# Expert weights of a pair in runs of 16 KiB, the second pair ranked beside `up`, and late transposes in the attention of a hybrid trunk

## The chip, the core and the metric

The kernel runs on one core of one Trainium2 chip. A core has five engines with queues of their own: TensorE (PE, with its weight loads as PEld), VectorE (DVE), ScalarE (ACT), GpSimd (POOL) and SyncE (SP), which here only issues transfers, and 16 DMA engines that carry them. The metric is the device time of one execution in microseconds; the number that counts is the median of repeated executions.

## What is computed

The reference is an encoder trunk of two layers on 512 tokens of 1024 values, all in float32. Cut to what matters:

```python
for i in range(DEPTH):                       # 2 layers
    proj = rmsnorm(h, g_mix[i]) @ w_in[i]    # 1024 x 2816: q, k, v of three head groups
    oa = axial_gqa(...)                      # a: 4 query heads, 2 key heads, normed and rotated q, k
    ob = neighbourhood_attn(...)             # b: 6 heads, 2-D window, learned bias
    oc = dilated_mixture(...)                # c: 6 heads, three dilated windows
    h = h + concat(rmsnorm each group) @ w_out[i]
    h = h + expert_choice_ffn(rmsnorm(h, g_ffn[i]), ...)
    h = h + sigmoid(rmsnorm(h, g_ple[i]) @ w_ple_gate[i]) * (p[i] @ w_ple_proj[i])

def expert_choice_ffn(h, w_router, w_gate, w_up, w_down):
    aff = softmax(h @ w_router)              # 16 experts
    gates, idx = top_k(aff.T, 64)            # each expert picks 64 tokens
    hid = silu(h[idx] @ w_gate) * (h[idx] @ w_up)     # 1024 x 1024 each, per expert
    return segment_sum((hid @ w_down) * gates, idx)
```

The weights of the experts are 3 x 16 matrices of 4 MiB in each layer, read once: 201 MB per layer. That is most of what the kernel loads.

## The kernel before

A layer goes through three stages. In **attention** the projection of the 2816 columns is cut into seven blocks in the order `cq, ck, cv, a, bq, bk, bv` (`IN_BLOCKS`, L36). A block is a `Project` (L355): eight steps of 128 input values, four token tiles in each, three products per step and tile, since operands are split into a high and a low half for the fast float32 format (`split`, L321: ACT makes the high half, POOL the low one). Work of VectorE and ScalarE is hung on the steps of a block by a dictionary from step to functions that `run` (L392) takes. So `post_qk` (L532) hands the norm and rotation of the q or k heads of the block before to steps 0 to 7 of this one: `chain` at step 0 makes the factors, `norm(t)` works on token tile t in place in the tile `raw` (four buffers, filled by `fin_qk`, L524, with a square and a copy on ACT), and `tr(t)` transposes the heads of tile t on PE into a buffer of the pair. `norm` has its operations in program order (`in_turn`, L513, its line in the profile is L515). Between the products of a block the units of the attention before it are emitted by `Side` (L167): each unit has a cost in microseconds, `step` grants credit for every product group at a pace, and `LEAD` (L42) is a cost that must be paid before the first unit of a group comes out. A scheduler then orders what is not pinned.

The **experts** work in eight pairs. For a pair, `gate`, `up` and `down` are four steps each (`expert_mm`, L1071); a step has 16 products of 64 columns by 512, the two experts j = 0, 1 in the two halves of the array. A pair's tokens are found by `choose` (L1044: `rank`, eight transposes of the affinities on PE and eight comparisons on VectorE, then four `pick`), `number` (L1022: the tokens' indices and gates by four products, each two matmul instructions in the trace) and `bring` (L1051: `number`, then an indirect transfer of the tokens' rows). Pair 0 instead gathers with products of one-hot matrices (`fetch`, L1036, the instructions `pick,h`). In pair 0, `number(0)` and `choose(1)` are done at gate step 2 and `bring(1)` at up step 1. The embedding stage follows, with `w_ple_gate` in four pieces.

All weights and many other long-lived tiles live in `Slots` (L89): 18 buffers of 8 KiB per partition, and in the expert stage three more lent from the pool `phY` (`NEARLY`, from the last part of the out-projection on) and two from `phX` (`NLENT`). A list made by `plan` (L244) gives the order of the loads. `pump` (L121) issues on SP whatever stands first as long as a buffer is free beyond a reserve, which `keep` (L134) sets at several points of attention (`KEEP`, L45); an expert load may also take a lent buffer. SP issues in order: a load whose buffer is not free yet, or whose completion counter (one of eight, used in turn) is still held by the eighth load before it, keeps those behind it waiting. One load of expert weights is a piece of two input blocks of one expert's matrix, 1 MiB, 8 KiB per partition in one run; a step needs two of them (j = 0, 1):

```python
for name, w in (("g", w_gate), ("u", w_up), ("d", w_down)):
    for i in range(4):
        for j in range(2):
            slots.want((l, name, e + j, i), [(lambda t: t, w[l, e + j, i])])
```

In the listing all products have the line of the helper `mm` (L210) and all transposes that of `transpose` (L213), so the profile tells them apart by their tiles.

## Time and profile before

| what | before |
|---|---|
| median of three executions | 1638.31 us |
| the three executions | 1637.62, 1638.31, 1642.08 us |
| the profiled execution | 1637.69 us |
| its span in the profile | 1635.9 us |
| PE busy | 1537.8 us (94%) |
| VectorE, ScalarE, GpSimd busy | 722.1, 474.9, 277.6 us |
| moved by DMA | 469.85 MB, mean 287 GB/s |
| loads of expert weights | 384 of 1024 KB, 19.8 us each from issue to landing |

The profiled execution's time is 1.8 us more than its span, which runs from the first to the last instruction. PE is busy most of the time, but a mean over stages hides that they have different limits: the slices of the page show 20 to 150 GB/s in attention and about 420 in the two expert stages. A busy PE also need not be PE at its peak, as the ends of matmuls are modelled. The time from issue to landing of a load contains the loads ahead of it in the DMA engines' queues. "x" and a number at the end of a timeline row counts the instructions merged into it, and a bracket gives the time for which the engine stood idle before, with what ended it.

### The profile page before, as it was taken

The numbers are of one execution on the slowest core, as the hardware profiler recorded it, in microseconds if no ns is written. First come the engines' busy times: TensorE is split into PE (matmuls) and PEld (weight loads), VectorE is DVE, ScalarE is ACT, GpSimd is POOL, SyncE is SP. The second block draws the span as 40 slices with busy tenths as digits, with TensorE's granted clock in tenths as the row PEclk, the third lists the DMA queues.
The fourth block names the chain that finished last, engine by engine and source line by source line (L and its number), as shares of the span: only waits on it lengthen the run. The fifth ranks groups of instructions, "written<-read, shape, count | busy, mean of one in ns | idle before, by whom it ended". The sixth has DMA issues, their size and how long they took to land.

```text
span 1635.9 us, 20629 instructions
## 1 busy us (share of the span) xinstructions
PE 1537.8 (94%) x7819; PEld 884.3 (54%) x7819; DVE 722.1 (44%) x1909; ACT 474.9 (29%) x1127; POOL 277.6 (17%) x282
## 2 busy tenths in 40 slices
PE   7999999899999888998999999998999997889988
PEld 7866777644343333333897667776344333333346
DVE  4767756443243222222476687554333242122143
ACT  6455544211010002012564645541101010021034
POOL 3413364000000000000443233620000000000013
PEclk9999999999999999999999999999999999999999
DMA  9103146899999999999420032387999999999961
GB/s 323 39 20 104 24 150 239 324 385 420 420 420 421 420 421 399 421 421 421 166 73 20 20 103 58 116 333 290 422 420 420 421 420 421 421 397 421 419 279 52
DMA packets 74691, 469.85 MB, mean 287 GB/s; under 512 B 10272, under 2 KB 13280, under 8 KB 23392
## 3 DMA queue, kind: packets, MB, share of 16 engines
q1 hardware_dynamic: 69808, 454.16, 69.5%
q0 software_dynamic: 3744, 13.16, 2.2%
q10 hardware_dynamic: 1040, 1.21, 0.3%
q8 instruction: 61, 1.00, 0.2%
q14 instruction: 38, 0.31, 0.1%
HBM read 461.04 MB, written 6.29 MB: 286 GB/s over the span
## 4 chain that ended last, share of the span: by engine, by line
PE 51%; DMA 32%; DVE 12%; ACT 3%; issue 1%; POOL 1%; SPq 0%; POOLq 0%; ACTq 0%; DVEq 0%
PE bank L210 47%; DMA slot<-in_w_up_dram 11%; DMA slot<-in_w_gate_dram 7%; DMA slot<-in_w_down_dram 7%; PE bank L213 4%; DVE raw L515 4%; DMA slot<-in_w_ple_proj_dram 3%; DMA slot<-in_w_ple_gate_dram 2%; DVE p L661 2%; DVE w L515 1%; DVE p L654 1%; ACT p L656 1%; DMA slot<-in_w_in_dram 1%; DMA gain<-in_qk_gain_dram 1%; DVE slot L682 1%
## 5 line engine op out<-in xcount | busy, mean ns | idle before, releaser
L210 PE MATMUL bank<-slot,xt 128*64 128x512 f32 x2048 | 464.7, 595 | 29.5 <-DMA slot<-in_w_up_dram 23.6
L210 PE MATMUL bank<-ch,slot 128*128 128x384 f32 (+1 forms) x2064 | 477.9, 374 | 2.1 <-DVE slot L332 1.8
L210 PEld LDWEIGHTS bank<-ch,slot 128*128 128x128 f32 x2064 | 361.0, 190 | 77.1 <-issue 40.2
L210 PEld LDWEIGHTS bank<-slot,xt 128*64 128x64 f32 x2048 | 147.4, 137 | 320.2 <-issue 260.6
L327 POOL TENSOR_TENSOR ch<-slot,ch 128x384 fp32r<-128x384 f32 (+1 forms) x172 | 200.0, 1169 | 351.2 <-ACT ch L326 341.4
L210 PE MATMUL bank<-slot,hid 128*64 128x512 f32 x1024 | 229.2, 595 | 13.9 <-DMA slot<-in_w_down_dram 10.9
L210 PEld LDWEIGHTS bank<-slot,hid 128*64 128x64 f32 x1024 | 76.0, 137 | 156.2 <-issue 125.9
L1165 DVE SCALAR_TENSOR_TENSOR hid<-bank,st,hid 128x512 f32<-128x512 f32 x32 | 24.0, 751 | 304.4 <-PE bank L210 302.5
L1055 POOL DMA_INDIRECT xg<-rows,ids x14 | 13.6, 971 | 727.5 <-DVE ids L1028 637.6
L210 PE MATMUL bank<-slot,slot 128*64 128x256 f32 (+4 forms) x688 | 129.1, 420 | 3.6 <-DVE sa L654 1.9
L326 ACT CAST ch<-slot 128x384 fp32r<-128x384 f32 (+1 forms) x172 | 95.8, 563 | 85.8 <-PE bank L210 68.9
L1202 DVE SCALAR_TENSOR_TENSOR xg<-bank,st,hid 128x512 fp32r<-128x512 f32 x32 | 22.6, 746 | 215.8 <-ACT hid L1201 215.8
L1100 DVE TENSOR_TENSOR h<-h,bank 128x512 f32<-128x512 f32 x128 | 79.8, 682 | 82.7 <-PE bank L210 82.7
L1161 ACT ACTIVATE hid<-bank,st 128x512 f32<-128x512 f32 x32 | 22.0, 687 | 264.5 <-PE bank L210 264.5
L210 PEld LDWEIGHTS bank<-slot,slot 128*64 128x64 f32 (+2 forms) x688 | 63.1, 160 | 50.9 <-issue 26.3
L1006 DVE SCALAR_TENSOR_TENSOR less<-bank,tgv,order 128x512 bf16<-128x512 f32 x128 | 87.6, 747 | 3.9 <-PE bank L213 3.9
L1067 ACT ACTIVATE xt<-bank,gcols 128x128 f32<-128x128 f32 x56 | 20.3, 367 | 213.5 <-PE bank L213 211.8
L1201 ACT ACTIVATE hid<-bank,st 128x512 fp32r<-128x512 f32 x32 | 20.2, 683 | 211.9 <-issue 145.4
L656 ACT ACTIVATE p<-p,sa 128x512 f32<-128x512 f32 (+1 forms) x96 | 58.7, 612 | 69.0 <-DVE sa L654 68.8
L332 DVE SCALAR_TENSOR_TENSOR slot<-bank,gcols,slot 128x128 fp32r<-128x128 f32 (+1 forms) x160 | 53.0, 372 | 42.2 <-ACT slot L331 42.0
L213 PE MATMUL bank<-ident,p 128*128 128x128 f32 x416 | 62.4, 273 | 5.1 <-ACT ot L720 3.0
L654 DVE CUSTOM_DVE_ANT_0 p<-bank,slot 128x512 f32<-128x512 f32 (+1 forms) x96 | 50.8, 549 | 35.4 <-PE bank L210 27.2
(135 smaller groups left out, 1384.7 us busy)
## 6 DMA issues: line engine op xcount, KB each, us to landing
slot<-in_w_gate_dram SPq DMA_DIRECT2D x128, 1024.0 KB, 19.8
slot<-in_w_up_dram SPq DMA_DIRECT2D x128, 1024.0 KB, 19.8
slot<-in_w_down_dram SPq DMA_DIRECT2D x128, 1024.0 KB, 19.8
slot<-in_w_in_dram SPq DMA_DIRECT2D x24, 768.0 KB, 15.0
slot<-in_w_ple_gate_dram SPq DMA_DIRECT2D x8, 1024.0 KB, 19.8
slot<-in_w_out_dram SPq DMA_DIRECT2D x6, 1024.0 KB, 6.4
slot<-in_w_in_dram SPq DMA_DIRECT2D x4, 1024.0 KB, 5.1
rows<-h POOLq DMA_DIRECT2D x8, 512.0 KB, 4.8
```

What stands on the lines that cost most here:

```text
L210: return placed(T.matmul(*a, **k))
L213: return placed(T.transpose(*a))
L326: S.copy(hi.bitcast(F32R), src)
L327: G.tensor_tensor(lo.bitcast(F32R), src, hi, ALU.subtract)
L332: V.scalar_tensor_tensor(lo.bitcast(F32R), b, g, hi, ALU.mult, ALU.subtract)
L515: tc.keep_in_program_order(V.tensor_tensor(*a))
L654: V.tensor_tensor_reduce(pv, in0=sv, in1=bias, scale=-1.0, scalar=3e38, op0=ALU.add, op1=ALU.min, accum_out=nm)
L656: S.activation(pv, pv, AF.Exp, bias=nm, scale=-1.0, accum_out=ls)
L661: V.tensor_scalar(pv, pv, r[:, i:i + 1], None, ALU.mult)
L1006: V.scalar_tensor_tensor(ph.pool.tile([128, 512], BF16, tag="less", name="less", bufs=2), bk[6 + j], aff[:, t, e:e + 1], order[:, 128 * (3 ...
L1100: V.tensor_tensor(h[:, t, 512 * c:512 * c + 512], h[:, t, 512 * c:512 * c + 512], b, ALU.add)
L1165: V.scalar_tensor_tensor(hid[:, c], bk[2 + c], rslot[:, pr:pr + 1], hid[:, c], ALU.mult, ALU.mult)
```

## The change

Three things are changed. First, the expert weights are laid out in DRAM by pair, so that one load brings step i of both experts, 2 MiB, with 16 KiB per partition in one run. `Slots` therefore holds nine buffers of 16 KiB, and one each from the two lent pools; other users get a half of such a buffer (`piece`), of a buffer that is opened either for loads and plain tiles (`f32`) or for tiles that hold rounded halves (`rounded`), and the buffer is free when both halves are. `keep` counts halves, with new reserves. Second, `choose(1)` moves from gate step 2 of pair 0 to up step 1, `number(0)` to gate step 3 and `bring(1)` to up step 2. Third, `post_qk` returns two dictionaries: `tr(2)` is at step 7 instead of 6, and `tr(3)` at step 1 of the block after; the numbers of `LEAD` grow.

```diff
@@ -39,12 +39,13 @@
 
 PACE = (1.0, 0.85, 0.8)
 
-LEAD = (0.5, 2.0, 3.0)
+LEAD = (3.5, 4.0, 4.0)
 BIAS_AT = 5
-
-KEEP = (9, 3, 2, 4)
-
-NEARLY, NLENT = 3, 2
+FIRST = 6
+
+KEEP = (11, 3, 2, 4)
+
+NEARLY, NLENT = 1, 1
 
 EMBED = 5
 
@@ -94,7 +95,8 @@
         self.nc = nc
         self.pool = pool
         self.lent = {}
-        self.free = list(range(NSLOT))
+        self.free = list(range(NSLOT // 2))
+        self.open = {}
         self.where = {}
         self.queue = []
         self.ready = {}
@@ -115,18 +117,29 @@
             self.free.remove(i)
         self.lent = {}
 
+    def fresh(self, i):
+        self.free.remove(i)
+        return self.lent.get(i, self.pool).tile([128, 2 * SLOT], F32, tag=f"slots{i}", name=f"slots{i}", bufs=1)
+
     def own(self):
-        return [i for i in self.free if i < NSLOT]
+
+        n = 2 * sum(i not in self.lent for i in self.free)
+        return n + sum(len(halves) for _, kind, halves in self.open.values() if kind == "f32")
 
     def pump(self):
         while self.queue and self.queue[0][0][0] <= self.layer:
-            ok = self.own() if len(self.own()) > self.reserve else []
+            spare = self.own() - self.reserve
             if self.queue[0][0][1] in ("g", "u", "d"):
-                ok = [i for i in self.free if i >= NSLOT or i in ok]
-            if not ok:
+                ok = [i for i in self.free if i in self.lent or spare > 1]
+                if not ok:
+                    return
+                t = self.fresh(ok[0])
+                self.where[id(t)] = (ok[0], None, t)
+            elif spare > 0:
+                t = self.piece("f32")
+            else:
                 return
             key, loads = self.queue.pop(0)
-            t = self.tile(ok[0])
             for view, src in loads:
                 self.nc.sync.dma_start(out=view(t), in_=src)
             self.ready[key] = t
@@ -147,20 +160,32 @@
     def done(self, key):
         self.give(self.ready.pop(key))
 
-    def tile(self, i):
-        self.free.remove(i)
-        t = self.lent.get(i, self.pool).tile([128, SLOT], F32, tag=f"slot{i}", name=f"slot{i}", bufs=1)
-        self.where[id(t)] = (i, t)
+    def piece(self, kind):
+        ok = [i for i, (_, k, halves) in self.open.items() if k == kind and halves]
+        if not ok:
+            ok = [i for i in self.free if i not in self.lent]
+            self.open[ok[0]] = (self.fresh(ok[0]), kind, [0, 1])
+        big, _, halves = self.open[ok[0]]
+        s = halves.pop(0)
+        t = big[:, SLOT * s:SLOT * s + SLOT]
+        self.where[id(t)] = (ok[0], s, t)
         return t
 
-    def take(self):
+    def take(self, kind="f32"):
         if self.reserve:
             self.reserve -= 1
-        return self.tile(self.own()[0])
+        return self.piece(kind)
 
     def give(self, *tiles):
         for t in tiles:
-            self.free.append(self.where.pop(id(t))[0])
+            i, s, _ = self.where.pop(id(t))
+            if s is not None:
+                halves = self.open[i][2]
+                halves.append(s)
+                if len(halves) < 2:
+                    continue
+                del self.open[i]
+            self.free.append(i)
         self.pump()
 
 
@@ -268,8 +293,7 @@
                 chunks(("pp",), w_ple_proj[l])
             for name, w in (("g", w_gate), ("u", w_up), ("d", w_down)):
                 for i in range(4):
-                    for j in range(2):
-                        slots.want((l, name, e + j, i), [(lambda t: t, w[l, e + j, i])])
+                    slots.want((l, name, e, i), [(lambda t: t, w[l, e // 2, i])])
         chunks(("ple",), w_ple_gate[l])
 
     ph = Phase("init")
...
@@ -585,7 +610,7 @@
                     V.tensor_copy(d, four(b)[:, 0:nh // 2, :])
 
             return {0: [chain], 1: [lambda: norm(0)], 2: [lambda: norm(1)], 3: [lambda: norm(2)],
-                    4: [lambda: norm(3), lambda: tr(0)], 5: [lambda: tr(1)], 6: [lambda: tr(2)], 7: [lambda: tr(3)]}
+                    4: [lambda: norm(3), lambda: tr(0)], 5: [lambda: tr(1)], 7: [lambda: tr(2)]}, {1: [lambda: tr(3)]}
 
         def fin_v(c0, dst):
             n = dst.shape[2]
@@ -705,9 +730,9 @@
                                self.pt(hp, s)[:, 256 * c:256 * c + 256], start=c == 0, stop=c == 3)
                 k = groups[self.kind][0] // 128 + pr["j"]
                 if k not in mt:
-                    if len(mt) % 2 == 0:
-                        mts.append(slots.take())
-                    u = four(mts[-1])
+                    if not mts:
+                        mts.extend(slots.take('rounded') for _ in range(4))
+                    u = four(mts[len(mt) // 2])
                     mt[k] = (u[:, 2 * (len(mt) % 2), :], u[:, 2 * (len(mt) % 2) + 1, :])
                 if self.kind not in og:
                     og[self.kind] = ph.tile(512, "squares")
@@ -774,13 +799,15 @@
         pj["cq"].run({4: [stats_h]}, pj["ck"])
         pinned[0] = False
         cqk = [slots.take()]
-        pj["ck"].run(post_qk(6, 0, 4, "c", 0, cqk[0]), pj["cv"])
+        now, late = post_qk(6, 0, 4, "c", 0, cqk[0])
+        pj["ck"].run(now, pj["cv"])
         cqk.append(slots.take())
         vct = slots.take()
         vc = vct[:, 0:1536].rearrange("q (t c) -> q t c", t=4)
         va = pa.tile(512, "va").rearrange("q (t c) -> q t c", t=4)
         layer.fin["cv"] = fin_v(0, vc)
-        pj["cv"].run(merge(post_qk(0, 6, 4, "c", 1, cqk[1]), {7: [gains_h]}), pj["a"])
+        now, then = post_qk(0, 6, 4, "c", 1, cqk[1])
+        pj["cv"].run(merge(late, now, {7: [gains_h]}), pj["a"])
         logn = slots.take()
         nc.sync.dma_start(out=four(logn), in_=cst_logn.rearrange("q (t k) -> q t k", t=4))
         ptx = [slots.take() for _ in range(2)]
...
@@ -857,7 +886,8 @@
             bias["fin"](t)
 
         layer.fin["bv"] = fin_vb
-        pj["bv"].run(merge(post_qk(0, 6, 2, "b", 0, bqk[1]), {BIAS_AT: [bias_b]}))
+        now, late = post_qk(0, 6, 2, "b", 0, bqk[1])
+        pj["bv"].run(merge(then, now, {BIAS_AT: [bias_b]}))
         vb = bias["v"]
         vsh = [ptx[1][:, 384 * i:384 * i + 384] for i in range(3)]
         for i in range(3):
@@ -940,9 +970,9 @@
               out_project("b", (2, 3, 4), 0, MAIN),
               out_project("b", (2, 3, 4), 1, FREE, last=(3, 4), fin=tail)]
         for i in range(4):
-            po[i].run(None, po[i + 1])
+            po[i].run(None if i else late, po[i + 1])
             if i % 2:
-                slots.give(mts.pop(0))
+                slots.give(mts[i // 2])
         side.drain()
         pa.close()
         phY = Phase("early", "right")
...
@@ -1072,15 +1102,14 @@
             for i in range(4):
                 for f in (at or {}).get(i, ()):
                     f()
-                ws = [slots.get((l, name, e + j, i)).rearrange("q (k f) -> q k f", k=2) for j in range(2)]
+                ws = slots.get((l, name, e, i)).rearrange("q (j k f) -> q j k f", j=2, k=2)
                 for kk in range(2):
                     k = 2 * i + kk
                     for c in range(2):
                         for j in range(2):
-                            mm(bk[banks[c]][64 * j:64 * j + 64, :], lhs(j, k), ws[j][:, kk, 512 * c:512 * c + 512],
+                            mm(bk[banks[c]][64 * j:64 * j + 64, :], lhs(j, k), ws[:, j, kk, 512 * c:512 * c + 512],
                                start=k == 0, stop=k == 7)
-                for j in range(2):
-                    slots.done((l, name, e + j, i))
+                slots.done((l, name, e, i))
 
         def slot_onehot(g, two):
 
@@ -1154,13 +1183,13 @@
                     at[2].append(lambda: bring(pr + 1))
             else:
                 at = {1: [second, lambda: fetch(0, (4, 5), 2)],
-                      2: [lambda: fetch(0, (6, 7), 3), lambda: number(0), lambda: choose(1)]}
+                      2: [lambda: fetch(0, (6, 7), 3)], 3: [lambda: number(0)]}
             expert_mm((0, 1), lambda j, k: xt[pr][:, k, 64 * j:64 * j + 64], e, "g", at)
             hid = halves(ph.tile(1024, "hid"))
             for c in range(2):
                 S.activation(hid[:, c], bk[c], AF.Silu, scale=rslot[:, pr:pr + 1])
             expert_mm((2, 3), lambda j, k: xt[pr][:, k, 64 * j:64 * j + 64], e, "u",
-                      {} if prev else {1: [lambda: bring(1)]})
+                      {} if prev else {1: [lambda: choose(1)], 2: [lambda: bring(1)]})
             for c in range(2):
                 V.scalar_tensor_tensor(hid[:, c], bk[2 + c], rslot[:, pr:pr + 1], hid[:, c], ALU.mult, ALU.mult)
             if 0 < pr < last_pair:
...
@@ -1305,7 +1334,10 @@
     w[:, :, 0:256] = w[:, :, 0:256].reshape(DEPTH, D, 2, 2, 64).transpose(0, 1, 3, 2, 4).reshape(DEPTH, D, 256)
     w = w.reshape(DEPTH, 2, 4, 128, IN_COLS).transpose(0, 1, 3, 2, 4)
     arrays["w_in"] = np.concatenate([w[..., c0:c0 + n].reshape(DEPTH, 2, 128, 4 * n) for _, c0, n in IN_BLOCKS], -1)
-    for n in ("w_gate", "w_up", "w_down", "w_ple_gate", "w_ple_proj"):
+    for n in ("w_gate", "w_up", "w_down"):
+        a = arrays[n].reshape(DEPTH, NE // 2, 2, 4, 2, 128, FF).transpose(0, 1, 3, 5, 2, 4, 6)
+        arrays[n] = np.ascontiguousarray(a).reshape(DEPTH, NE // 2, 4, 128, 4 * FF)
+    for n in ("w_ple_gate", "w_ple_proj"):
         a = arrays[n]
         a = a.reshape(a.shape[:-2] + (a.shape[-2] // 256, 2, 128, D))
         arrays[n] = np.ascontiguousarray(a.swapaxes(-3, -2)).reshape(a.shape[:-3] + (128, 2 * D))
```

The places in the queues that matter, as they stand in program order. On SP, between the loads of `w_out` and the first weights of pair 0 in layer 0 (`slot` and `slots` are the buffers of `Slots`, the numbers tell allocations apart; 128x2048 is 1 MiB). Before:

```order
L131 DMA slot_2051<-in_w_gate_dram 128x2048
L848 DMA slot_1980<-in_cst_maskb_dram 128x256 x2
L131 DMA slot_2055<-in_w_gate_dram 128x2048
L131 DMA slot_2053<-in_w_gate_dram 128x2048
L131 DMA slot_2163<-in_w_gate_dram 128x2048
L131 DMA slot_2320<-in_w_gate_dram 128x2048
L131 DMA slot_2514<-in_w_up_dram 128x2048
L131 DMA slot_2419<-in_w_gate_dram 128x2048
L131 DMA slot_2508<-in_w_gate_dram 128x2048
L131 DMA slot_2510<-in_w_gate_dram 128x2048
L131 DMA slot_2516<-in_w_up_dram 128x2048
```

Now:

```order
L144 DMA slots_2025<-in_w_gate_dram 128x4096
L144 DMA slots_2486<-in_w_gate_dram 128x4096
L144 DMA slots_2482<-in_w_gate_dram 128x4096
L144 DMA slots_2484<-in_w_gate_dram 128x4096
L144 DMA slots_2488<-in_w_up_dram 128x4096
L144 DMA slots_2490<-in_w_up_dram 128x4096
L144 DMA slots_2496<-in_w_up_dram 128x4096
L144 DMA slots_2560<-in_w_up_dram 128x4096
L144 DMA slots_2695<-in_w_down_dram 128x4096
L144 DMA slots_2713<-in_w_down_dram 128x4096
```

The masks of the neighbourhood attention have moved ahead of this place, each load is twice as large, the second to fourth loads of gate wait for buffers that were taken after the first one's, and all of gate stands ahead of up.

On PE, at the end of the `ck` block of layer 0 and the start of `cv`, the transposes of the q heads of `c` (`raw` is the head tile, `ident` the identity, bank 64 to 67 the four tiles' sums). Before, the third and the fourth:

```order
L210 MATMUL bank_67<-ch,slot_106 128x384 x2
L210 MATMUL bank_67<-ch,slot_108 128x384
L213 MATMUL bank_71<-ident,raw 128x128 x3
L210 MATMUL bank_64<-ch,slot_106 128x384 x2
L210 MATMUL bank_64<-ch,slot_108 128x384
L213 MATMUL bank_68<-ident,raw 128x128 x3
L210 MATMUL bank_64<-ch,slot_106 128x384 x2
L210 MATMUL bank_64<-ch,slot_108 128x384
```

Now, the fourth, in `cv`:

```order
L235 MATMUL bank_64<-ch,slots_105 128x384
L235 MATMUL bank_65<-ch,slots_104 128x384 x2
L235 MATMUL bank_65<-ch,slots_105 128x384
L235 MATMUL bank_66<-ch,slots_104 128x384 x2
L235 MATMUL bank_66<-ch,slots_105 128x384
L238 MATMUL bank_68<-ident,raw 128x128 x3
L235 MATMUL bank_64<-ch,slots_104 128x384 x2
L235 MATMUL bank_64<-ch,slots_105 128x384
L235 MATMUL bank_65<-ch,slots_104 128x384
L235 MATMUL bank_67<-ch,slots_104 128x384 x2
L235 MATMUL bank_67<-ch,slots_105 128x384
```

Before, three products lie between the third and the fourth; now the fourth comes behind the nine products of tiles 0 to 2 in the first step of `cv`. The sum of `ck` in bank 67 is copied into the `raw` buffer that this transpose reads, and the first product of `cv` into that bank stands four products behind it.

On PE, at pair 0 in layer 0 (`pick` are one-hot columns, `tgv` the affinities with the token numbers, `xt` the gathered tokens). Before, between gate step 1 and gate step 2:

```order
L210 MATMUL bank_67<-pick,h 128x128 x8
L210 MATMUL bank_71<-tgv,pick 128x18 x4
L213 MATMUL bank_70<-ident,tgv 128x128 x4
L213 MATMUL bank_71<-ident,tgv 128x128 x4
L210 MATMUL bank_64<-slot_2320,xt 64x512
L210 MATMUL bank_64<-slot_2419,xt 64x512
L210 MATMUL bank_65<-slot_2320,xt 64x512
L210 MATMUL bank_65<-slot_2419,xt 64x512
```

Now, from the end of gate step 2 on:

```order
L235 MATMUL bank_64<-slots_2484,xt 64x512 x2
L235 MATMUL bank_65<-slots_2484,xt 64x512 x2
L235 MATMUL bank_71<-tgv,pick 128x18 x4
L235 MATMUL bank_64<-slots_2486,xt 64x512 x2
L235 MATMUL bank_65<-slots_2486,xt 64x512 x2
L235 MATMUL bank_64<-slots_2486,xt 64x512 x2
L235 MATMUL bank_65<-slots_2486,xt 64x512 x2
L235 MATMUL bank_66<-slots_2488,xt 64x512 x2
L235 MATMUL bank_67<-slots_2488,xt 64x512 x2
L235 MATMUL bank_66<-slots_2488,xt 64x512 x2
L235 MATMUL bank_67<-slots_2488,xt 64x512 x2
L238 MATMUL bank_70<-ident,tgv 128x128 x4
```

The products of `number(0)` stand behind gate step 2, and the eight transposes that rank the second pair behind the first step of up.

## Rows read from the trace of the kernel before

**Rows 1.** The page's part 4: the chain that ended last, by engine.
```profile
PE 51%; DMA 32%; DVE 12%; ACT 3%; issue 1%; POOL 1%; SPq 0%; POOLq 0%; ACTq 0%; DVEq 0%
```

**Rows 2.** Chain of waits, pieces in time: start us, us, engine and tile.
```profile
403.12 2.77 PE bank L213 x24
...
452.72 2.77 PE bank L213 x24
...
473.86 21.12 DMA slot<-in_w_up_dram
...
754.85 16.93 DMA slot<-in_w_ple_gate_dram
...
1282.43 21.09 DMA slot<-in_w_up_dram
```

**Rows 3.** Windows: us, busy per engine (PE, PEld, DVE, ACT, POOL), PEclk, DMA share, GB/s.
```profile
15.00:23.00 8.00, 8.00 (x43) 7.88 (x43) 4.55 (x16) 4.58 (x15) 0.00 (x0) 1.00 1.02 419
313.00:320.00 7.00, 6.77 (x37) 4.76 (x37) 2.70 (x9) 0.37 (x1) 0.00 (x0) 0.79 0.66 279
321.00:331.00 10.00, 9.93 (x70) 6.78 (x71) 1.66 (x8) 1.61 (x5) 0.00 (x0) 1.00 0.83 320
335.00:755.00 420.00, 396.14 (x1817) 156.78 (x1815) 119.64 (x339) 43.79 (x84) 6.79 (x7) 0.99 1.01 418
640.00:740.00 100.00, 98.02 (x434) 37.92 (x434) 18.82 (x47) 11.20 (x20) 0.96 (x1) 1.00 1.01 421
1143.00:1561.00 418.00, 393.47 (x1808) 155.48 (x1806) 119.91 (x341) 43.78 (x84) 6.80 (x7) 0.99 1.01 417
```

**Rows 4.** Timeline of SP's queue, layer 0: start us, us, line, tile, count.
```profile
207.58 0.34 SPq L131 DMA_DIRECT2D slot<-in_w_gate_dram  x1
...
212.62 22.55 SPq L131 DMA_DIRECT2D slot<-in_w_gate_dram  x4
...
256.13 7.74 SPq L131 DMA_DIRECT2D slot<-in_w_gate_dram  x3
268.54 10.45 SPq L131 DMA_DIRECT2D slot<-in_w_up_dram  x7
...
321.23 20.35 SPq L131 DMA_DIRECT2D slot<-in_w_gate_dram  x8
```

**Rows 5.** Waits of PE, 36 to 300 us, then 844 to 1108: total us, times, longest.
```profile
PE bank L213 <- DVE raw L515: 3.8, 3, 2.0
...
PE bank L213 <- DVE slot L682: 1.4, 2, 1.1
...
PE bank L213 <- DVE raw L515: 3.4, 3, 2.0
```

**Rows 6.** Timeline of PE, end of the cv block, layer 0; in brackets idle before.
```profile
68.30 0.55 PE L213 MATMUL bank<-ident,raw 128*128 128x128 f32 x3 [0.41 <-DVE raw L515]
68.60 0.78 PE L210 MATMUL bank<-ch,slot 128*128 128x384 f32 x3
71.39 0.55 PE L213 MATMUL bank<-ident,raw 128*128 128x128 f32 x3 [2.01 <-DVE raw L515]
71.69 3.60 PE L210 MATMUL bank<-ch,slot 128*128 128x384 f32 x19
```

**Rows 7.** Timeline of ACT in the ck block, layer 0.
```profile
55.17 0.49 ACT L529 COPY raw<-bank 128x384 f32<-128x384 f32 x1
```

**Rows 8.** Timeline of PE, gate steps 1 to 3 of pair 0, layer 0.
```profile
328.61 0.96 PE L210 MATMUL bank<-tgv,pick 128*128 128x18 f32 x8
329.43 1.35 PE L213 MATMUL bank<-ident,tgv 128*128 128x128 f32 x8
330.71 10.52 PE L210 MATMUL bank<-slot,xt 128*64 128x512 f32 x48
```

**Rows 9.** The page's part 5: VectorE's comparisons that rank the tokens (L1006).
```profile
L1006 DVE SCALAR_TENSOR_TENSOR less<-bank,tgv,order 128x512 bf16<-128x512 f32 x128 | 87.6, 747 | 3.9 <-PE bank L213 3.9
```

**Rows 10.** Timeline of POOL: the last split of w_out, layer 0.
```profile
281.10 1.30 POOL L327 TENSOR_TENSOR ch<-slot,ch 128x512 fp32r<-128x512 f32 x1 [0.81 <-ACT ch L326]
```

More of the change, by code (lines that the diff above doesn't have):

```diff
@@ L107, in lend @@
     def lend(self, pool, n):
-        first = NSLOT + len(self.lent)
+        first = NSLOT // 2 + len(self.lent)
         self.lent.update({i: pool for i in range(first, first + n)})
@@ L450, in __init__ @@
             self.l = l
-            self.xs = [slots.take() for _ in range(4)]
+            self.xs = [slots.take('rounded') for _ in range(4)]
             self.fin = {}
@@ L484, in trunk @@
         pj, xs = layer.pj, layer.xs
-        slots.keep(3)
+        slots.keep(FIRST)
         slots.keep(KEEP[0])
@@ L803, in trunk @@
         layer.fin["a"] = fin_a
-        pj["a"].run(None, pj["bq"])
+        pj["a"].run(then, pj["bq"])
         aqk = slots.take()
-        pj["bq"].run(post_qk(4, 2, 0, "a", 0, aqk), pj["bk"])
+        now, late = post_qk(4, 2, 0, "a", 0, aqk)
+        pj["bq"].run(now, pj["bk"])
         side.drain()
@@ L818, in trunk @@
         slots.keep(KEEP[2])
-        pj["bk"].run(post_qk(6, 0, 2, "b", 1, bqk[0]), pj["bv"])
+        now, then = post_qk(6, 0, 2, "b", 1, bqk[0])
+        pj["bk"].run(merge(late, now), pj["bv"])
         bqk.append(slots.take())
@@ L955, in trunk @@
         router_mm(3)
-        slots.give(*mts)
+        slots.give(*mts[2:])
         if stop == "attn":
@@ L1218, in wg_at @@
             return at
-        wt = slots.take()
+        wt = slots.take('rounded')
         first = [split(wg_at(0)(k), 512, wt[:, 1024 * k:1024 * k + 1024]) for k in range(2)]
         combine(*prev, (0, 1), MAIN)
-        es = [slots.take() for _ in range(4)]
+        es = [slots.take('rounded') for _ in range(4)]
         last = l == depth - 1
```

## The prediction

> **What bounds the kernel now.** I read the chain of waits by engine first, then its pieces in order of time, then the windows, the queue of SP, the waits of PE, and last the timelines at the places that the change touches. By engine the chain is PE for half of the span and DMA for a third [rows 1], and its pieces say where each rules [rows 2]: in layer 0 a pair of experts takes 49.6 us as long as PE sets the pace (two transposes of `hid` lie at 403.12 and 452.72), but from 473.86 to 754.85 the chain consists of DMA pieces of 20 to 21 us, and the gate weights of the embedding end it at about 771.8. Layer 1 does the same from 1282.43 on. The windows show why [rows 3]: the DMA engines are busy all the time (share 1.01) at 417 to 421 GB/s. A pair is 24 slots of 1.049 MB, 25.2 MB, which take 59.8 us at 421 GB/s, 10 us more than PE needs. So the end of an expert stage is set by the bytes still to come when the stream becomes saturated, divided by the rate. That happens at about 335 in layer 0 (the two windows before it are at 279 and 320 GB/s, with holes) and at about 1143 in layer 1. Two things can move it: the rate, and how many megabytes have landed by then. What shortens attention shifts everything behind it and counts in full, since the buffers come free by PE's progress there.
>
> **The change, part by part.** *Runs of 16 KiB.* No row here has a run above 8 KiB, so the rate is extended from the two lengths that saturate the engines: `w_in`, 6 KiB, at 419 GB/s, and the expert weights, 8 KiB, at 421 [rows 3]. Sixteen engines at these rates spend 6144 x 16 / 419 = 234.6 ns and 8192 x 16 / 421 = 311.3 ns on a run, 76.7 ns for 2 KiB more. Then 16 KiB take 311.3 + 4 x 76.7 = 618.1 ns, an estimate: 424.1 GB/s, 0.74% more. On the 420 and 418 us of the two saturated stretches that is 3.1 us each, **-6.2 us**. The rows are rounded to 1 GB/s; with 418.5 and 421.5 the gain is 1.1% (-9.2 us), with 419.5 and 420.5 it is 0.35% (-2.9 us). Nothing in the trace excludes a loss above 8 KiB; I take +2.9 us, the smallest gain turned round, as the upper end. I take the middle value, because the two rows measure the same queue in the same run. [...] Halving the number of expert DMAs gives nothing else: the queue of SP is idle most of the time.
>
> *Transposes one block later.* PE waits three times in each layer for the last multiplications of a norm (VectorE, L515) before a transpose: 3.8 us in layer 0, 3.4 in layer 1 [rows 5]. The timeline shows two of them, 0.41 us before the third transpose of the k heads of `c` and 2.01 us before the fourth, 0.78 us of products between them [rows 6]. The change puts the third three products later, 0.6 us at the 0.19 us of one (19 in 3.60), and the fourth behind the rest of the block and nine products of the next, some 30 or 5.7 us; both are more than the waits, so all 7.2 us can go. It adds a wait: `raw` has four buffers, and in `ck`, `bq` and `bk` ScalarE's copy of the block's own last tile into the fourth now waits for that late transpose, which reads the heads of the block before. Queued behind the copy are ScalarE's casts of weight halves, and the first product of the block after into that PSUM bank waits for it as well. The copy takes 0.49 us [rows 7]; after the transpose PE has four products, 0.75 us, before it needs the bank. So it costs nothing if ScalarE is free, and up to 0.7 us if a cast of 0.5 us goes first. Three blocks in each of two layers: 0 to 4.2 us, of which I take 2.2 us, the middle. Net **-5.0 us** (ends -7.2 and, with the rival on this below, about 0). The longer lead only shifts units of attention to where PE has as many products left; I cost it at nothing, and what covers it is the drain at the end of the `bq` block.
>
> *Where the prefetch starts.* Big buffers come free only when both halves are free, and `keep` holds more back early. In the order of SP only one `w_gate` stands ahead of the tiles of the neighbourhood attention now, and a second waits for their last reader; in the trace of before five were issued by 235, and the next three at 256 to 264 [rows 4]. The other tiles of pair 0 follow in places where the kernel before issues the rest of `w_up` (268.5 to 279 [rows 4]): from about 271 on. Between 271 and 321 the stream must then carry nine big tiles, 18.9 MB, and 2.1 MB of rows written for the gather: 21.0 MB or 49.9 us at 421 GB/s. That just fits, with no slack, whereas before it had run dry between 313 and 321 (279 GB/s) [rows 3]. In exchange the buffers are 22 slots, not 23: 1.05 MB less in store when saturation begins, +2.5 us per layer. Against that stands the moved ranking: before, PE does 0.96 us of `number` and 1.35 us of transposes between gate steps 1 and 2 of pair 0 [rows 8], and the buffers of step 2 come free that much later, while the stream is not yet full; -2.3 us per layer. I add 1 us per layer for holes at issues that come just as the stream runs out. Net +1.2 per layer, **+2.0 us** rounded for the kernel (ends -2 and +8, if holes take 4 us per layer).
>
> *The ranking beside `up`.* Eight comparisons of 0.747 us [rows 9] and four picks, some 6.5 us on VectorE, now have one step of 16 products (3.65 us at the pace of gate steps, 48 in 10.52 [rows 8]) before `bring(1)` needs them; before, they had all of steps 2 and 3 and one more. PE will stall for about 3 us in up step 2, and the buffers behind it come free 3 us late. The stream covers this: by then PE frees 2.1 MB every 3.5 us, where the stream takes 5.0 us for them, and four steps have passed since 321. So 0; with the cover gone, +2 us per layer.
>
> The sum is -6.2 - 5.0 + 2.0 = -9.2 us. Against the profiled execution, 1637.69 us, that is **1628.5 us**; the profiled run is 0.6 us under the median of the three runs, 1638.31. What a measurement can tell from no change is 0.3%, 4.9 us.
>
> **The rivals.** *The rate does not move.* Long runs are carried as fast as 8 KiB ones, because the engines are already as busy as they get (share 1.01 at 421, 1.02 at 419). For it: 419 against 421 is close to the rounding. Against it: the longer run is the faster one in every window that I looked at. By this mechanism the time is -5.0 + 2.0: 1634.7 us. [...]
>
> *The waits of attention come back elsewhere.* The copy into `raw` costs its full 0.7 us six times, and the shifted units of `c` meet a VectorE that is busier, doubling waits like those for the evacuation of transposes (1.4 us in a layer [rows 5]). Then -7.2 + 4.2 + 2.8 is about 0, and the time is -6.2 + 2.0: 1633.5 us. Against it: most of these waits are shorter than the work that can be put ahead of them.
>
> *The prefetch starts too late* (the other side: slower). The nine tiles between 271 and 321 have no slack, so every microsecond by which their first is late, in both layers, adds 2 us. From 4.6 us per layer on the kernel is slower than before, from 7.4 on by more than 0.3%. The nearest row for such a slip is the last split of `w_out` on POOL, which ends at 282.40 [rows 10]: a queue that is held up to there, since SP issues in order and one unfreed half keeps all that follows, is 11.4 us late, and the time 1628.5 + 22.8 = 1651.3 us. For it: SP's order now has that split's buffers ahead of four `w_down`. Against it: the buffers before these belong to blocks that end before 271.
>
> **How the numbers follow.** The forecast has 0.57: faster by over 0.3% in 0.52 of it, within 0.3% in 0.05 (thin rate gain with more holes). The unmoved rate has 0.17: 0.05 faster (if attention gives its full 7.2 us), 0.12 within. The waits that come back have 0.13: 0.05 faster, 0.08 within. The late prefetch has 0.13: 0.10 slower, 0.03 within. Together 0.62 faster, 0.28 same, 0.10 slower. The range: the best ends of the three terms together are -9.2 - 7.2 - 2 = -18.4, 1619.3 us; I set 1618. Upwards it takes in the rivals at 1633.5 and 1634.7 and holes of 4 us per layer on top of the latter (+6, 1640.7), so 1641; left out is most of the late prefetch.
>
> **What would show it.** Right: windows in the middle of the expert stages at 424 GB/s, DMA pieces of the chain twice as long, the line of waits for L515 gone from attention, the cores of both expert stages ending 3 us after shorter saturated stretches, PE reaching the first `w_gate` product some 2.5 us earlier per layer. Wrong: 421 GB/s again; holes in the DMA row between 271 and 330; a wait of PE for `raw` (L529 of before) or for picks that is followed by a hole in the stream; PE still waiting for L515.

## The result, and the profile of the changed kernel

| what | before | changed |
|---|---|---|
| median | 1638.47 us (4 runs) | 1620.42 us (4 runs, 1619.73 to 1622.36) |
| ratio | | 0.9888 (95% interval 0.987 to 0.9905) |
| profiled execution, span | 1637.69, 1635.9 us | 1620.56, 1618.7 us |
| DMA packets | 74691 | 47039 |

The changed kernel is 18 us faster, 1.1%. The forecast was 1628.5 us with a range of 1618 to 1641: the side and the signs of the three terms were right, and each term was about half of what was measured.

The windows of the changed kernel that answer to [rows 3], with the same columns (us, busy per engine in the order PE, PEld, DVE, ACT, POOL, then the clock of PE, the DMA share and GB/s):

```profile
15.00:23.00 8.00, 8.00 (x47) 7.87 (x46) 5.23 (x17) 5.41 (x17) 0.00 (x0) 1.00 1.02 418
271.00:313.00 42.00, 37.80 (x233) 31.07 (x233) 20.05 (x53) 13.21 (x32) 7.31 (x11) 0.92 0.98 406
320.00:335.00 15.00, 15.00 (x82) 6.66 (x80) 1.84 (x12) 2.00 (x4) 0.00 (x0) 1.00 0.99 395
335.00:755.00 420.00, 392.62 (x1830) 153.36 (x1826) 123.11 (x345) 42.41 (x82) 6.79 (x7) 0.99 1.01 424
640.00:740.00 100.00, 96.10 (x443) 35.12 (x441) 19.14 (x48) 8.27 (x15) 0.97 (x1) 1.00 1.01 427
1143.00:1561.00 418.00, 390.51 (x1807) 151.72 (x1804) 116.33 (x321) 44.05 (x85) 7.85 (x8) 0.99 1.01 424
```

The saturated stream runs at 427 GB/s where it ran at 421, 1.4% more, with the DMA engines as busy as before (share 1.01); the forecast had 424. The stream has been nearly full since 271 (406, then 395 GB/s), where the kernel before had holes (279 and 320 in [rows 3]). Only four of the loads of pair 0 are issued in the 52 us from 221.78 on, the rest from 274 on, as SP's queue shows (start and length in us, of the loads merged into a row):

```profile
221.78 52.26 SPq L144 DMA_DIRECT2D slots<-in_w_gate_dram  x4
274.13 4.19 SPq L144 DMA_DIRECT2D slots<-in_w_up_dram  x4
295.63 21.05 SPq L144 DMA_DIRECT2D slots<-in_w_down_dram  x4
322.36 13.91 SPq L144 DMA_DIRECT2D slots<-in_w_gate_dram  x4
```

PE no longer waits for the norm in attention. What it waits for there, most first, in 30 to 300 us (the three lines of [rows 5] are of 36 to 300 and 844 to 1108):

```profile
PE bank L235 <- ACT raw L553: 1.9, 3, 0.7
PE bank L238 <- ACT slots L608: 1.1, 1, 1.1
PE bank L235 <- DVE slots L610: 0.8, 1, 0.8
PE bank L235 <- DVE sa L679: 0.7, 1, 0.7
```

The wait for L515 (3.8 us) is gone; the wait for the copy into `raw` that the change adds is there, three waits of at most 0.7 us, 1.9 us in all, and the same in layer 1. Its place in layer 0, on PE and on ACT at the end of the `ck` block:

```profile
53.87 0.49 PE L238 MATMUL bank<-ident,raw 128*128 128x128 f32 x3
54.12 0.94 PE L235 MATMUL bank<-ch,slots 128*128 128x384 f32 x4
55.77 2.54 PE L235 MATMUL bank<-ch,slots 128*128 128x384 f32 x13 [0.70 <-ACT raw L553]
```

```profile
54.87 0.22 ACT L319 ACTIVATE sa<-sa 128x24 f32<-128x24 f32 x1 [1.36 <-DVE sa L569]
55.12 0.22 ACT L320 ACTIVATE sa<-sa 128x24 f32<-128x24 f32 x1
55.25 0.46 ACT L553 COPY raw<-bank 128x384 f32<-128x384 f32 x1
```

The late transpose ends at 54.36, but the copy starts at 55.25: it stands in ACT's order behind the two small activations of the next chain, and these wait for VectorE until 54.87. That is where this wait of 0.7 us comes from, and not from a cast.

The three stretches of the time can be read from two tiles. `xt` gives the first product of the experts and `hid` the last product with `w_down` (the rows give duration in ns as min/median/max, then the first and the last start in us). Before, layer 0, then layer 1:

```profile
L210 PE MATMUL bank<-slot,xt x1024: 592/592/644, 317.1 to 747.9; 128*64 128x512 f32 x171
L210 PE MATMUL bank<-slot,hid x512: 592/592/644, 355.1 to 767.8; 128*64 128x512 f32 x171
...
L210 PE MATMUL bank<-slot,xt x1024: 592/592/643, 1125.7 to 1556.5; 128*64 128x512 f32 x171
L210 PE MATMUL bank<-slot,hid x512: 592/592/643, 1163.6 to 1576.4; 128*64 128x512 f32 x171
```

Changed:

```profile
L235 PE MATMUL bank<-slots,xt x1024: 592/592/1115, 312.7 to 739.8; 128*64 128x512 f32 x171
L235 PE MATMUL bank<-slots,hid x512: 592/592/643, 352.7 to 759.4; 128*64 128x512 f32 x171
...
L235 PE MATMUL bank<-slots,xt x1024: 592/592/1113, 1111.5 to 1539.7; 128*64 128x512 f32 x171
L235 PE MATMUL bank<-slots,hid x512: 592/592/644, 1151.6 to 1559.3; 128*64 128x512 f32 x171
```

From the start to the first expert product: 317.1 to 312.7, -4.4 us. The expert stage of layer 0, from there to the last `w_down` product: 450.7 to 446.7, -4.0. From that to the first expert product of layer 1: 357.9 to 352.1, -5.8. The stage of layer 1: 450.7 to 447.8, -2.9. The rest is as long as before (1635.9 - 1576.4 and 1618.7 - 1559.3). Together -17.1 of the 17.2 us that the span lost: 10.2 in attention and what is around it, 6.9 in the expert stages.

How much of the 10.2 us is waiting can be read from PE's busy time in the two stretches outside the expert stages, before and then changed:

```profile
0.00:317.10 317.10, 293.97 (x1706) 231.56 (x1706) 205.21 (x535) 160.05 (x404) 112.05 (x121) 0.99 0.43 151
767.80:1125.70 357.90, 343.29 (x1949) 271.03 (x1947) 235.34 (x596) 190.52 (x474) 131.05 (x131) 0.99 0.37 133
```

```profile
0.00:312.70 312.70, 293.10 (x1708) 232.54 (x1708) 204.72 (x535) 160.34 (x404) 113.34 (x121) 0.99 0.40 141
759.40:1111.50 352.10, 341.20 (x1949) 270.70 (x1945) 236.28 (x596) 190.21 (x474) 132.57 (x131) 0.99 0.34 123
```

PE stands idle for 23.1 and 14.6 us before, for 19.6 and 10.9 us now: 7.2 us less. The other 3.0 us are busy time, 0.9 and 2.1 us, for the same work.

### The profile page after: what moved, and what is told of

Same layout as the page of the kernel before. It is cut to its first block, busy times and chain, and to the rows that moved or that the text cites. A ratio compares the mean times of both kernels' runs of the same rounds, so it can differ in the third digit from the quotient of the medians.

```text
span 1618.7 us, 20230 instructions
## 1 busy us (share of the span) xinstructions
PE 1524.3 (94%) x7819; PEld 875.3 (54%) x7819; DVE 722.5 (45%) x1909; ACT 475.1 (29%) x1127; POOL 280.5 (17%) x282
## 2 busy tenths in 40 slices
DMA packets 47039, 469.81 MB, mean 290 GB/s; under 512 B 7200, under 2 KB 10208, under 8 KB 20320
## 5 line engine op out<-in xcount | busy, mean ns | idle before, releaser
L235 PE MATMUL bank<-slots,xt 128*64 128x512 f32 x2048 | 458.9, 600 | 30.3 <-DMA slots<-in_w_up_dram 22.4
L235 PE MATMUL bank<-ch,slots 128*128 128x384 f32 (+1 forms) x2064 | 471.3, 372 | 5.9 <-ACT raw L553 3.8
L235 PEld LDWEIGHTS bank<-ch,slots 128*128 128x128 f32 x2064 | 360.3, 189 | 80.5 <-issue 37.4
L235 PEld LDWEIGHTS bank<-slots,xt 128*64 128x64 f32 x2048 | 142.6, 138 | 316.5 <-issue 264.7
L351 POOL TENSOR_TENSOR ch<-slots,ch 128x384 fp32r<-128x384 f32 (+1 forms) x172 | 201.2, 1176 | 314.6 <-ACT ch L350 309.4
L235 PE MATMUL bank<-slots,hid 128*64 128x512 f32 x1024 | 225.9, 595 | 13.4 <-DMA slots<-in_w_down_dram 10.3
L235 PEld LDWEIGHTS bank<-slots,hid 128*64 128x64 f32 x1024 | 71.7, 137 | 156.5 <-issue 137.7
L350 ACT CAST ch<-slots 128x384 fp32r<-128x384 f32 (+1 forms) x172 | 95.6, 562 | 94.0 <-PE bank L235 68.3
L235 PE MATMUL bank<-slots 64*128 64x512 f32 (+2 forms) x304 | 95.0, 556 | 1.3 <-DVE sa L679 1.3
L686 DVE TENSOR_SCALAR p<-p,sa 128x512 f32<-128x512 f32 (+1 forms) x128 | 63.2, 509 | 3.4
## 6 DMA issues: line engine op xcount, KB each, us to landing
slots<-in_w_in_dram SPq DMA_DIRECT2D x4, 1024.0 KB, 11.4
```

The source lines that it names most:

```text
L235: return placed(T.matmul(*a, **k))
L350: S.copy(hi.bitcast(F32R), src)
L351: G.tensor_tensor(lo.bitcast(F32R), src, hi, ALU.subtract)
L686: V.tensor_scalar(pv, pv, r[:, i:i + 1], None, ALU.mult)
```

## The experiments

All are edits of the changed kernel, except where the kernel before is named. Each was timed beside the kernel before on its own chip, where that took 1637.7 to 1638.1 us; a difference from the changed kernel's 1620.42 us is one between chips. The ratios are to the kernel before, with their 95% intervals.

### The rate: length of a run, or number of loads

The same loads of 2 MiB, but the halves of the two experts apart in DRAM:

```diff
-slots.want((l, name, e, i), [(lambda t: t, w[l, e // 2, i])])
+slots.want((l, name, e, i), [(lambda t: t.rearrange("q (j x) -> q j x", j=2),
+                              w[l, e // 2, i].rearrange("j q x -> q j x"))])
...
-a = arrays[n].reshape(...).transpose(0, 1, 3, 5, 2, 4, 6)
+a = arrays[n].reshape(...).transpose(0, 1, 3, 2, 5, 4, 6)
...
```

> The changed kernel, but the two experts' halves of a 2 MiB load lie apart in DRAM, so that a partition is written by two runs of 8 KiB; number and size of loads, buffers and order stay. Theory 1 (the length of a run sets the rate): the stream falls from 427 back to 421 GB/s, 1.4% on two stretches of some 418 us, about 6 us per layer: 1632 us. Theory 2 (the number of loads, each with its end, sets the rate): 427 GB/s stay, 1620 us. Half of each would give 424 GB/s and 1626 us.

Measured: 1633.19 us (ratio to before 0.9972, 0.9961 to 0.9983), and the stream back at 421:

```profile
640.00:740.00 100.00, 95.75 (x434) 35.45 (x434) 18.82 (x47) 9.68 (x18) 0.97 (x1) 1.00 1.01 421
```

Its expert stages take 452.7 and 453.2 us, 6.0 and 5.4 more than in the changed kernel. The number, size and order of the loads are the changed kernel's; so it is the run's length. Then the same layout with two loads of 1 MiB for each buffer:

```diff
+slots.want((l, name, e, i), [(lambda t, j=j: t[:, SLOT * j:SLOT * j + SLOT], w[l, e // 2, i, j])
+                              for j in range(2)])
```

> The changed kernel, each big buffer filled by two loads of 1 MiB with runs of 8 KiB, as the kernel before loads them; buffers, order and attention as changed. Both theories of the rate: 421 GB/s, about 1632 us, which leaves 6 us of the 18 to attention and entry together; if the time is nearer to 1626 the rate is not the larger half of the gain.

Measured: 1633.55 us (0.9968, 0.9956 to 0.9981), 420 and 421 GB/s in the windows at 640 and 400. Twice as many loads cost nothing that can be measured. Of the 18 us the rate holds 13, the rest 5: it is the larger half.

The other way round, long runs in small loads, first with the lower and the upper 64 partitions:

```diff
+slots.want((l, name, e, i), [(lambda t, s=s: t[64 * s:64 * s + 64, :],
+                              w[l, e // 2, i, 64 * s:64 * s + 64]) for s in range(2)])
```

> The changed kernel, each 2 MiB load cut into two of 64 partitions, 1 MiB each, with runs of 16 KiB; 384 loads of expert weights as in the kernel before. Theory 1 (run length): 427 GB/s and 1620 us. Theory 2 (number of loads): 421 GB/s, 1632 us.

Measured: 2468.57 us, which neither theory had. This is the median of four executions between 2324 and 2521 us; the profiled one took 2431.82 us. The window at 400 to 600:

```profile
400.00:600.00 200.00, 120.48 (x412) 44.62 (x408) 30.75 (x92) 8.85 (x18) 1.93 (x2) 0.79 1.01 219
```

The DMA engines are as busy as ever (1.01) and move half as much. This run says nothing on the two theories, since it changed something else: where a load lands. Nor is it that a load reads 1 MiB of DRAM in one piece, for the kernel before does so at 421 GB/s. The next one takes every second partition, and so spreads each load over the whole range again:

```diff
+slots.want((l, name, e, i), [(lambda t, s=s: t[s::2, :], w[l, e // 2, i, s::2]) for s in range(2)])
```

> The changed kernel, each 2 MiB load cut into two of 64 partitions as in the run that took 2469 us, but the even and the odd partitions instead of the lower and the upper half: 384 loads of 1 MiB, runs of 16 KiB. If the neighbourhood of the 64 partitions halved the rate there (219 GB/s, 1186 ns for a run of 16 KiB where 613 ns were taken), it is whole again: 427 GB/s, and with theory 1 (run length) 1620 us, with theory 2 (number of loads) 421 GB/s and 1632 us. If any load to 64 partitions is slow: 219 GB/s and 2450 us again.

Measured: 1625.71 us (0.9924, 0.9907 to 0.9941), and the rate of the changed kernel with the number of loads of the kernel before:

```profile
640.00:740.00 100.00, 97.21 (x441) 36.22 (x441) 18.81 (x47) 9.45 (x17) 0.97 (x1) 1.00 1.01 427
```

Theory 1 has the rate. The time is 5 us above the 1620 that it gives. In the trace 0.3 us of this lie before the first expert product, 2.0 and 1.5 in the two stages (448.7 and 449.3 us) and 1.2 between them; the rate in the saturated stretch is whole, and why small loads cost this here and not with runs of 8 KiB stays open.

### Attention

The kernel before with the late transposes and the longer leads alone (the two dictionaries of `post_qk`, its five calls, and `LEAD`, as in the diff of the change):

> The kernel before with the late transposes and the longer leads alone. Theory 3 (attention alone brought the first expert product forward, 4.5 us in layer 0 and 5.7 more in layer 1): 1638.4 - 10 = 1628 us. Rival (only the waits for the norm less the new waits for the copy into raw count, 3.7 - 1.9 us in layer 0 and the like in layer 1; the rest came with the order of the buffers): 1638.4 - 3.6 = 1635 us.

Measured: 1627.98 us (0.9939, 0.9922 to 0.9956). Theory 3: attention alone is 10.1 us, twice what was forecast. The stages of this run take 450.7 and 450.8 us, as in the kernel before, so all of it lies in front of them. From the other side, the changed kernel with the transposes put back (`tr(2)` at step 6, `tr(3)` at 7, the five calls as before), first with the longer leads:

> The changed kernel with all four transposes of a block's heads back in the block they were in, the longer leads kept. [...] Theory 3b (the leads bring nothing by themselves): 1620.4 + 10 = 1630.5 us.

Measured: 1631.56 us (0.9958, 0.9942 to 0.9975). Then with the shorter leads too:

```diff
-LEAD = (3.5, 4.0, 4.0)
+LEAD = (0.5, 2.0, 3.0)
```

> The changed kernel with the attention of the kernel before: transposes back and the shorter leads. Theory 3b (the leads bring nothing by themselves): as with the longer leads, 1630 to 1632 us, so that the late transposes alone are the 10 us. Theory 3d (the longer leads cost something where the transposes are early, about 3 us per layer as the last products of the blocks come that much later in that run): 1625 us. With the leads bringing half of it: 1636 us.

Measured: 1632.91 us (0.9971, 0.9961 to 0.9981). The two do not differ beyond their intervals: where the transposes are early, the leads bring nothing (3b), and, with the longer leads, the late transposes are worth 11 us here. In the first of the two the wait for the norm is back in both layers:

```profile
PE bank L238 <- DVE raw L539: 3.4, 3, 2.0
```

and in layer 0 PE's granted clock falls in the stretch behind its longest wait, the one of 2.0 us at 70, where the changed kernel has full speed. The window from 72 to 100, of this run, then of the changed kernel:

```profile
72.00:100.00 28.00, 28.00 (x131) 19.94 (x132) 12.46 (x38) 13.87 (x30) 7.72 (x6) 0.95 0.20 61
```

```profile
72.00:100.00 28.00, 28.00 (x136) 18.25 (x135) 14.92 (x42) 13.47 (x31) 8.49 (x7) 1.00 0.19 61
```

At 0.95 of full speed 28 us hold 26.6 us of work: 1.4 us lost beside the wait itself, 1.7 if the end of the wait, from 70 on, is taken in. The kernel before has the same in layer 1, 1.7 us in the two windows around and behind the wait:

```profile
875.00:880.00 5.00, 2.60 (x14) 2.23 (x14) 4.46 (x11) 1.14 (x3) 1.27 (x1) 0.91 0.08 32
880.00:885.00 5.00, 5.00 (x23) 4.59 (x22) 0.00 (x0) 2.82 (x6) 0.42 (x1) 0.75 0.00 0
```

So a wait of 2 us can cost PE another 1.7 us after it, which no list of waits shows. It does not always: the same pair of waits, 0.4 and 2.0 us, stands in both layers of the four kernels with early transposes, and the clock falls behind it in five of the eight places and not in the other three. Layer 0 of the kernel before is one of the three; there the wait ends at 71.39, in the first of these windows:

```profile
70.00:75.00 5.00, 3.61 (x22) 3.61 (x23) 2.39 (x8) 1.54 (x3) 0.00 (x0) 1.00 0.01 3
75.00:80.00 5.00, 5.00 (x22) 3.33 (x21) 2.20 (x8) 3.55 (x9) 2.54 (x2) 1.00 0.00 0
```

The window from 70 to 75 of the run above, with the transposes put back and the longer leads:

```profile
70.00:75.00 5.00, 3.10 (x11) 3.10 (x12) 2.90 (x8) 0.58 (x1) 0.48 (x1) 0.66 0.01 3
```

What tells the five from the three no run here shows. The last run on attention gives `raw` one buffer more:

```diff
-raw[t] = pa.tile(384, "raw", 4)
+raw[t] = pa.tile(384, "raw", 5)
```

> The changed kernel with five buffers for raw instead of four, so that the copy of a block's last tile no longer waits for the late transpose. Theory 3c (the three waits of 0.7 us per layer that the change added stand on the path): 1620.4 - 3.8 = 1616.6 us, and the waits of PE for the copy are gone. Rival (ScalarE or the next wait takes their place): 1619 to 1621 us.

Measured: 1619.18 us (0.9888, 0.9872 to 0.9905), 1.2 us under the changed kernel and not to be told from it by the intervals. The wait for the copy is gone from both layers. Part of it comes back elsewhere, as the rival says: PE now waits for an evacuation of attention's transposes, in layer 0 and then in layer 1:

```profile
PE bank L238 <- ACT slots L705: 0.7, 1, 0.7
...
PE bank L238 <- ACT slots L705: 1.4, 2, 0.7
```

The first expert product comes 0.9 us earlier in layer 0 (311.8), and the way from the last `w_down` product to layer 1's first is 1.0 us shorter (351.1): 1.9 of the 3.8 us.

### Entry into the expert stage

The ranking back in its old place:

```diff
-      2: [lambda: fetch(0, (6, 7), 3)], 3: [lambda: number(0)]}
+      2: [lambda: fetch(0, (6, 7), 3), lambda: number(0), lambda: choose(1)]}
-      {} if prev else {1: [lambda: choose(1)], 2: [lambda: bring(1)]})
+      {} if prev else {1: [lambda: bring(1)]})
```

> The changed kernel with number(0) and choose(1) back at gate step 2 of pair 0 and bring(1) at up step 1. Theory 4 (the buffers of gate step 2 come free 2.3 us later while the stream is not full, so each expert stage ends 2.3 us later): 1625 us. Rival (the stream's backlog covers it, and the stall of 1.7 us for the picks goes): 1620 us or a little less.

Measured: 1621.84 us (0.9906, 0.9889 to 0.9922), 1.4 us above the changed kernel, inside the intervals. The stages take 447.4 and 447.3 us, against 446.7 and 447.8. The rival holds: the stream is a little less full where the buffers come later (365 instead of 395 GB/s at 320 to 335), but the end of the stage doesn't move by the 2.3 us that were counted.

```profile
320.00:335.00 15.00, 14.93 (x86) 7.14 (x84) 8.11 (x32) 2.00 (x4) 0.00 (x0) 1.00 0.92 365
```

One lent buffer of 16 KiB less, 20 slots' worth instead of 22:

```diff
-NEARLY, NLENT = 1, 1
+NEARLY, NLENT = 1, 0
```

> The changed kernel with one lent big buffer instead of two: 20 slots' worth instead of 22. Theory 5 (what is in store when the stream becomes saturated sets the end of the stage; 2.1 MB at 427 GB/s are 4.9 us per layer): 1630.2 us, from which the one slot that the change gave up (23 to 22) cost 2.5 us per layer. Rival (the start of the prefetch sets it, the last buffers come too late to matter): 1620 to 1622 us.

Measured: 1632.6 us (0.9968, 0.9957 to 0.9978), 12 us above the changed kernel where 9.8 were worked out; its stages take 453.2 and 453.0 us, 6.5 and 5.2 more. And the kernel before with as many buffers as the change leaves:

```diff
-NEARLY, NLENT = 3, 2
+NEARLY, NLENT = 3, 1
```

> The kernel before with one lent buffer less, 22 buffers of 8 KiB instead of 23, as many as the change leaves. Theory 5 (1.05 MB less in store at the start of saturation, 2.5 us per layer at 421 GB/s, or 3 us by the run with 20): 1643 to 1644 us. Rival (the last buffer is never filled in time, so it is worth nothing): 1638 us.

Measured: 1641.67 us (1.0024, 1.0015 to 1.0034). Its rows of `xt` and `hid` in layer 0, and in layer 1:

```profile
L210 PE MATMUL bank<-slot,xt x1024: 592/592/643, 317.5 to 750.8; 128*64 128x512 f32 x171
L210 PE MATMUL bank<-slot,hid x512: 592/592/644, 355.5 to 770.7; 128*64 128x512 f32 x171
...
L210 PE MATMUL bank<-slot,xt x1024: 592/592/643, 1128.7 to 1561.8; 128*64 128x512 f32 x171
L210 PE MATMUL bank<-slot,hid x512: 592/592/1065, 1166.6 to 1581.7; 128*64 128x512 f32 x171
```

The stages are 453.2 and 453.0 us long, 2.5 and 2.3 more than with 23 buffers. By the medians this run is 3.9 us above the kernel before on its chip, where 1643 to 1644 us, some 5 us, were expected; by the stages 4.8. Theory 5: what is in store when the stream becomes saturated counts in full, 1.05 MB as 2.5 us at 421 GB/s.

## Why the prediction was right, and where its sizes were off

**What bounds the kernel.** Right: the expert stages end by bytes over rate. The two runs with fewer buffers and the two with runs of 8 KiB all move the stage's end by what that division gives, to within 1.6 us, while PE's products in them stay the same.

**The rate: -6.2 us forecast, some -11 to -13 measured.** The mechanism was right, and the rival that the rate doesn't move is excluded by the run with 8 KiB in loads of 2 MiB. The step that failed is the size taken from the two rates 419 and 421. With 427 GB/s a run of 16 KiB takes 16384 x 16 / 427 = 613.9 ns, two of 8 KiB at 421 take 622.6: a run has 8.7 ns of its own, an estimate from the two rates (7 to 10 by their rounding), where the forecast's line gives 4.5. The row of 6 KiB that I drew the line through is a window of 8 us, whose value is 410 to 419 in the runs of this study, a spread larger than the whole difference that was to be read from it; the ends that I gave, 0.35% and 1.1%, took in only the rounding and missed 1.4% too. By the stages the rate is worth 6.0 and 5.4 us, by the medians 12.8.

**Attention: -5.0 us forecast, -10.1 measured.** All three waits for the norm in each layer went, 7.2 us over both, as worked out. The new wait was sized at 2.2 us and is 3.8, near its upper end of 4.2, and for another reason than the cast: the copy stands behind activations that wait for VectorE. The step that failed is the new order of the units, costed at nothing, and beside it the granted clock, which no term had. Other waits changed too: outside the two lines of `raw` PE waited 5.6 us in layer 0 before ([rows 5] shows one of these lines, 1.4 us), and the changed kernel has some 3.3 us. In layer 1 these lines go from 5.5 to 3.5. By the list, then, the waits change by -7.2 + 3.8 - 4.3 = -7.7 us; by PE's idle time in the two stretches it is -7.2. And the granted clock: the stretch of lower clock behind the long wait of layer 1 (0.91 and 0.75 of full speed in the windows from 875 to 885, 0.50 from 880 to 882) went with the wait, 1.7 us; the changed kernel has 1.00 from 860 to 895. Of the 10.2 us by which the changed kernel's trace is shorter there, 7.2 are idle time and 1.7 the clock; the remaining 1.3 us of busy time are not accounted for. Since the clock does not fall behind every such wait, these 1.7 us are in part the luck of the profiled execution. Which of the other waits goes with the transposes and which with the leads was not tried apart: the shorter leads with late transposes would read heads that are not yet transposed.

**Entry: +2.0 us forecast, +4.5 measured** (the stages of the run with 8 KiB runs against those of the kernel before, 2.0 and 2.5 us longer at the same 421 GB/s). The capacity step was right, 2.5 us forecast and 2.5 and 2.3 measured. With the two layers together 4.8, it is the whole term. The step that failed is the 2.3 us per layer that the moved ranking should give back: putting it back costs 0.7 and -0.5 us. The prediction counted a hole in the stream of the kernel before ([rows 3], 320 GB/s) as if the changed kernel had it too, but there the stream is nearly full at that time. The holes that were added, 1 us per layer, don't show either (406 GB/s from 271 on). A slip of the sum lies beside it: 1.2 us per layer are 2.4 for the kernel, which was put at 2.0.

**The stall for the picks.** Right: PE waits 1.7 us for them in up step 2 (forecast about 3), and nothing behind it moves. The step that the ranking has to itself was put at 3.65 us; its row, 48 products in 10.52 us, gives 3.5.

**The rivals.** The late prefetch did not come: `w_up` is issued from 274 on, close to the 271 worked out. The waits that return elsewhere came in half: the copy at its full price, but with fewer other waits, not more.

The three measured terms, -11.4 (stages of the run with 8 KiB against the changed kernel), -10.1 and +4.5, give -17.0, and the medians differ by 18.05. That the time still lies in the range, 2.4 us above its lower end, is luck in part: the rate and attention each gave more than the best end worked out for them (-9.2 and -7.2), together -21.5 us, and without the entry's 2.5 us above the forecast the time would have come to the range's edge.

## What to carry to other kernels

Where a stream is at the DMA engines' limit, look at the length of the contiguous run before anything else (here 421 GB/s with 8 KiB, 427 with 16), and price it from a long saturated window or from a run that changes only the layout; a line through a short window can be off by its whole slope. In such a stage, as here (2.3 to 2.5 us for 1.05 MB, 5.2 to 6.5 for 2.1 MB), a megabyte of buffer is worth about its transfer time once per stage, so a layout that needs larger buffers must be charged for the buffer that no longer fits. And a wait of TensorE of 2 us may cost 1.7 us more behind it, when the granted clock falls, as it did in five places of eight: read the clock of the stretch after a wait before pricing its removal.

## What the runs showed of the hardware that I had not expected

Loads of 1 MiB into partitions 0 to 63 and 64 to 127 in turn move 219 GB/s (400 to 600 us) with the DMA engines busy all the time; loads of the same size into the even and the odd partitions move 427. A run of 16 KiB then takes about 16384 x 16 / 219 = 1197 ns, an estimate from the rate (the expectation above had 1186), instead of 614. Two loads that together fill all partitions did not add up, though some eight were under way in one queue, an estimate: a load there takes 37.5 to 39.7 us from issue to landing (medians for the three matrices), in which 219 GB/s move 8.2 to 8.7 MB. In the changed kernel's trace, too, none of the 267 transfers on SP behind the first eight is issued before the eighth ahead of it has landed, and 96 of them are issued within 0.1 us of that. Why these partitions halve the rate was not shown. Nor is it a fixed half: with the same loads and the engines as busy, the rate rises to 240 GB/s at 1000 to 1100 us and, in layer 1, from 222 at 1600 to 1800 to 284 at 2200 to 2300. Why it rises stays open.
